# A streaming-encoder kernel: idle products at the start, x on another queue, a new order of the first splits

## The chip, the cores and the metric

The kernel runs on one core of a Trainium2 chip. A core has five engines that run at the same time, each doing its own instructions strictly in their order: TensorE (PE in the profile; PEld are its weight loads), VectorE (DVE), ScalarE (ACT), GpSimd (POOL) and SyncE (SP). Engines wait for each other, and for transfers (DMA), by semaphores. The metric is the device time of one execution in microseconds (us); less is better.

## What is computed

Two layers over 256 positions of width 1024, each of three sub-layers with a layer norm behind each. The first and third sub-layer are gated feed-forward parts with 2816 inner channels, the second is a diagonal state-space mixer (S5) in layer 0 and a gated spatial mixer in layer 1. Everything is float32.

```python
def _swiglu(x, w_in, w_out):
    gate, up = jnp.split(x @ w_in, 2, axis=-1)
    return (jax.nn.silu(gate) * up) @ w_out

for i in range(2):
    h = _layernorm(ALPHA * h + 0.5 * _swiglu(h, ffn_w_in[i, 0], ffn_w_out[i, 0]), ...)
    mix = _s5_mixer(h, ...) if i == 0 else _gmlp_mixer(h, ...)
    h = _layernorm(ALPHA * h + mix, ...)
    h = _layernorm(ALPHA * h + 0.5 * _swiglu(h, ffn_w_in[i, 1], ffn_w_out[i, 1]), ...)

# in the S5 mixer, from its small parameters
dt = jnp.exp(log_dt)                       # step sizes
mag = jnp.exp(a_re * dt); lam = mag * (cos(a_im * dt), sin(a_im * dt))
bbar = (lam - 1) / a * b                   # then a scan over positions with lam
```

## The kernel before

**Products in two parts.** Each float32 operand is split into a high part (a cast, on ACT) and a low part (the difference, on DVE), and a product is two or three PE products of parts: high by high, high by low, low by high. So each weight has to pass ACT and DVE before PE can use it.

**The weight stream.** Class `Stream` brings all weights in blocks of 128 x 2048 values (1 MB), numbered here from 0 in the order of use. `load` issues a block's transfers on SP's queue into one of three raw buffers (`N_RAW`); a raw buffer is free again when its block's low part is made. `split` makes the parts, into one of five pairs of split buffers (`N_SPLIT`), free again when PE has used the block. `tick` is called by the program after each group of PE products: it finishes what is unfinished, loads, splits up to n blocks, and does one step of background work. With `lazy` set, a tick casts the high part and leaves the low part to the next tick.

**The first feed-forward sub-layer** goes in eleven chunks of 256 inner channels. The blocks are: 0 and 1 for chunk 0, 2 and 3 for chunk 1, 4 and 5 for chunk 2, then for each further chunk c one block of the output weights of chunk c - 3 and two of its input weights: 6, then 7 and 8 for chunk 3, and so on to 24, then 25 and 26 for chunk 9. `start_in` does chunk 0 by itself, in quarters of a block as they come in (lines named L106 and L107 in the profile, `split_pieces`): it turns x by PE transposes (`make_xt`, L187, parts on ACT and DVE at L192 and L193) and multiplies (`in_mm`, L201 to L203, one group of three products for each of the eight slices k of the width and each half t of the positions). Then `chunk_in(1)` and onward, whose products are the lines L208 to L210, four groups of 24 products a chunk, each group followed by a tick; from chunk 2 on each chunk is followed by the output products of the chunk two before it (`step_out`).

**x.** Its first 128 positions (`h[0]`) are loaded by SP in two halves ahead of the weights; the second 128 (`h[1]`) stand among the quarters of block 0, behind its second quarter.

**The preparation of the S5 mixer** runs as background work under this first sub-layer, a list of steps (`add(first, cost, f)`): a step is done in order when the count of ticks has reached `first` and credit is left. It begins with `turn_a`, called as `ws.early` in `start_in`: small PE transposes of the parameters (L751, L752) and copies of them on ACT (L748 to L763). Then come the exponential for the step sizes `dt` in three pieces on DVE (L717, L721), `scaled` on POOL (L711, `ch<-ch,dt`), 32 small loads of B and 16 of C issued by POOL (L908, L977), rotation factors by repeated squaring on POOL (`seed`), a base table on POOL (`base_table`), rows for B on DVE (`b_rows`, with factors that go out to memory and come back by `spread`), and from tick 20 on tables made on DVE from a copy of the base table on ACT (`table`, L887 is that copy `tb<-base`), then products (`product`, `pq`).

The order of all this is fixed by the program as written; nothing is planned while it runs.

Of the kernel before, what the change touches and what calls it, by code (L numbers as in the profile page):

```python
# [9 lines left out]
F32 = mybir.dt.float32  # L10
# [6 lines left out]
P = 128  # L17
# [137 lines left out]
def hybrid(ctx: ExitStack, tc: tile.TileContext, a: dict, out: bass.AP, subs=SUBS):  # L155
# [186 lines left out]
    def plan_ffn(li, fi, fine):  # L342
        w_in, w_out = a["ffn_w_in"][li, fi], a["ffn_w_out"][li, fi]
        ids = {"in": {}, "out": {}}

        def add_in(c):

            ids["in"][c] = []
            for kh in range(2):
                parts = []  # L350
                step = 1 if fine and c == 0 else 4
                for k in range(0, 4, step):
                    row = 512 * kh + P * k
                    src = w_in[row:row + P * step, :].rearrange("(k p) (g n) -> p k g n", p=P, g=2)[:, :, :, c * FC:c * FC + FC]
                    dst = lambda raw, k=k, step=step: raw.rearrange("p (k g n) -> p k g n", k=4, g=2)[:, k:k + step]
                    if step == 1:
                        parts.append((lambda raw, dst=dst: dst(raw)[:, 0], src[:, 0]))
                    else:
                        for g in range(2):
                            parts.append((lambda raw, dst=dst, g=g: dst(raw)[:, :, g], src[:, :, g]))  # L360
                if step == 1 and kh == 0:
                    parts[2:2] = [(lambda raw: h[1], a["x"][0, P:2 * P, :])]
                ids["in"][c].append(ws.add(*parts))

        add_in(0)
        add_in(1)
        for c in range(2, NCH):
            add_in(c)
            ids["out"][c - 2] = add_rows(w_out, (c - 2) * FC)
        for c in (NCH - 2, NCH - 1):  # L370
            ids["out"][c] = add_rows(w_out, c * FC)
        return ids

    def ffn(ids, li, si, first, last):
# [42 lines left out]
        def chunk_in(c):  # L417

            for m in range(2):
                ps = mm_p.tile([P, 2, SEQ], F32, tag="mm", name="ips")  # L420
                for g in range(2):
# [10 lines left out]
                        finish_g()  # L432
                    if (m, g) == (1, 1) and c == NCH - 1:
                        split_gt()
                    ws.tick()

        def chunk_in2(c):

# [34 lines left out]
        def split_gt():  # L473
            while later:
                x, g = later.pop()
                nc.scalar.copy(x[:, 0], g)  # L476
                nc.vector.tensor_tensor(x[:, 1], g, x[:, 0].bitcast(F32), op=ALU.subtract)  # L477

        def start_in():

            ps = [mm_p.tile([P, 512], F32, tag="mm", name="ips") for _ in range(2)]
            mm = lambda t, k: in_mm(ids["in"][0], t, ps[t], [k])
            make_xt(0, parts=[0])
            split = ws.split_pieces(4)
            split(0)
            make_xt(0, parts=[1])
            mm(0, 0)
            split(1)
            make_xt(1)
            ws.early()  # L490
            mm(0, 1)
            for k in range(2):
                mm(1, k)
            for k in range(2, 4):
                split(k)
                for t in range(2):
                    mm(t, k)
            split = ws.split_pieces(4)
            for k in range(4):
                split(k)  # L500
                for t in range(2):
                    mm(t, 4 + k)
                if k >= 2:
                    ws.tick(0)
# [23 lines left out]

        if first:
            start_in()  # L530
            ws.lazy = True
            chunk_in(1)
        else:
            step_in(0, 0, split=0)
# [157 lines left out]
    def prepare_s5(sm, qp, dram):  # L692
# [326 lines left out]
        loads()  # L1019
        ws.early = turn_a  # L1020
        for cost, f in exp(lambda: val["ldt"], "dt"):
            add(1, cost, f)
        add(2, 0, scaled)
        for part in range(4):
            add(2, 0, load_b, part)
# [334 lines left out]
    with tc.manual_schedule():  # L1360
# [8 lines left out]
        kinds = [k for k, _, _ in subs]  # L1369
        for n in range(2):  # L1370
            s = slice(512 * n, 512 * n + 512)
            nc.sync.dma_start(out=h[0][:, s], in_=a["x"][0, 0:P, s])
        if kinds[0] != "ffn":
            nc.sync.dma_start(out=h[1], in_=a["x"][0, P:2 * P, :])
        ws.fill()
        if kinds[0] != "ffn":
            make_xt(0, kinds[0] == "s5")
# [52 lines left out]
```

## Time and profile before

| | us |
|---|---|
| median of 3 runs | 956.26 |
| lowest, highest | 956.1, 958.12 |
| profiled execution | 957.04 |
| its span in the profile | 955.2 |

| engine | busy, share of the span |
|---|---|
| PE | 937.7 us, 98% |
| DVE | 693.5 us, 73% |
| ACT | 466.9 us, 49% |
| POOL | 155.7 us, 16% |

In rows in order of time the first number is the start in us from the span's start, the second the duration (of all instructions that the row merges, from the first's start to the last's end), then engine, line, operation, output<-input, the shape and the count. Behind it, in brackets, stands how long the engine had been idle and what released it. In a row of a stretch, each engine's busy us stand in the order that the row above names, then the granted PE clock and the transfers. A row of waits gives who waited for whom, the sum, how often and the longest. A row of transfers ends with the KB of one and the median us from issue to landing.

### The profile page before, as it was taken

How to read it: one execution, taken by the hardware profiler on the slowest of the kernel's cores; microseconds unless marked ns; L12 is line 12 of the kernel's file. 1: busy time of each engine (PE TensorE's matmuls, PEld its weight loads, DVE VectorE, ACT ScalarE, POOL GpSimd, SP SyncE). 2: the span in 40 equal slices, each digit the busy share in tenths (PEclk: the TensorE clock that was granted, in tenths of full speed). 3: DMA queues.
4: the chain of work that ended last, by engine and by line, in shares of the span. 5: the costliest groups of instructions: out<-in, count | busy, mean ns of one | idle time of the engine just before them, and what ended most of it. 6: DMA issues, size and time to landing. Idle time of an engine off the chain costs nothing.

```text
span 955.2 us, 15164 instructions
## 1 busy us (share of the span) xinstructions
PE 937.7 (98%) x6142; PEld 813.9 (85%) x6142; DVE 693.5 (73%) x930; ACT 466.9 (49%) x612; POOL 155.7 (16%) x228
## 2 busy tenths in 40 slices
PE   7999999999999999999999999999999999999996
PEld 6999999978898888888888888888889888888885
DVE  6789998787999766564677756556789867564655
ACT  5475347534334464545534645454445445545540
POOL 1878911001652000000001000000000000000000
PEclk9999999999999999999999999999999999999999
DMA  8787696858637657465557674646357467565521
GB/s 280 208 244 251 219 313 218 293 202 322 221 124 242 197 178 248 149 215 181 176 176 243 222 262 161 228 140 221 132 176 265 132 201 233 184 219 178 182 84 45
DMA packets 134038, 195.02 MB, mean 204 GB/s; under 512 B 7648, under 2 KB 104848, under 8 KB 133968
## 3 DMA queue, kind: packets, MB, share of 16 engines
q1 hardware_dynamic: 129296, 182.74, 58.1%
q0 software_dynamic: 4384, 10.92, 3.9%
q8 instruction: 48, 0.79, 0.3%
q10 hardware_dynamic: 288, 0.39, 0.1%
q14 instruction: 22, 0.18, 0.1%
HBM read 184.07 MB, written 9.96 MB: 203 GB/s over the span
## 4 chain that ended last, share of the span: by engine, by line
PE 75%; DVE 2%; ACT 1%; POOL 0%; issue 0%; DVEq 0%; POOLq 0%; ACTq 0%
PE ips L216 21%; PE ips L217 11%; PE acc L203 8%; PE acc L201 8%; PE acc L202 8%; PE ips L203 2%; PE ips L201 2%; PE ips L202 2%; PE pps L1152 2%; PE tps L187 1%; PE zps L210 1%; PE zps L209 1%; PE zps L208 1%; PE ups L203 1%; PE ups L201 1%; PE ups L202 1%
## 5 line engine op out<-in xcount | busy, mean ns | idle before, releaser
L216 PE MATMUL ips<-xt,hi 128*128 128x512 f32 x864 | 306.2, 398 | 0.0
L89 DVE TENSOR_TENSOR lo<-raw,hi 128x2048 fp32r<-128x2048 f32 x107 | 243.1, 2294 | 8.2 <-ACT hi L88 8.0
L217 PE MATMUL ips<-xt,lo 128*128 128x256 f32 x864 | 242.5, 281 | 0.0
L88 ACT CAST hi<-raw 128x2048 fp32r<-128x2048 f32 x107 | 204.3, 1912 | 43.8 <-PE acc L203 25.3
L216 PEld LDWEIGHTS ips<-xt,hi 128*128 128x128 f32 x864 | 162.3, 188 | 39.9
L217 PEld LDWEIGHTS ips<-xt,lo 128*128 128x128 f32 x864 | 163.1, 189 | 1.1
L201 PE MATMUL acc<-hi,gt 128*128 128x512 f32 x346 | 136.2, 394 | 0.5 <-ACT gt L476 0.5
L451 DVE TENSOR_TENSOR sgg<-sgg,ips 128x256 f32<-128x256 f32 x108 | 45.5, 421 | 124.5 <-ACT sgg L450 124.1
L203 PE MATMUL acc<-hi,gt 128*128 128x512 f32 x346 | 135.1, 391 | 0.0
L202 PE MATMUL acc<-lo,gt 128*128 128x512 f32 x346 | 134.9, 390 | 0.0
L229 POOL TENSOR_TENSOR rstd<-rstd,mhalf 128x1 f32<-128x1 f32 x14 | 13.3, 950 | 619.7 <-DVE rstd L228 619.7
L97 DVE TENSOR_TENSOR lo<-raw,hi 128x2048 fp32r<-128x2048 f32 (+2 forms) x52 | 89.8, 1754 | 24.8 <-ACT hi L96 24.6
L450 ACT COPY sgg<-ips 128x256 f32<-128x256 f32 x108 | 40.3, 373 | 115.7 <-PE ips L217 115.7
L210 PE MATMUL ips<-xt,lo 128*128 128x256 f32 x320 | 90.7, 284 | 2.1 <-DVE lo L89 2.1
L208 PE MATMUL ips<-xt,hi 128*128 128x256 f32 x320 | 90.8, 284 | 0.0
L209 PE MATMUL ips<-xt,hi 128*128 128x256 f32 x320 | 90.5, 283 | 0.0
L201 PEld LDWEIGHTS acc<-hi,gt 128*128 128x128 f32 x346 | 65.0, 188 | 14.7 <-ACT gt L476 1.3
L203 PEld LDWEIGHTS acc<-hi,gt 128*128 128x128 f32 x346 | 64.9, 188 | 14.7 <-DVE gt L477 0.3
L96 ACT CAST hi<-raw 128x2048 fp32r<-128x2048 f32 (+2 forms) x52 | 74.9, 1484 | 2.6 <-DMA raw<-in_ffn_w_in 2.3
L202 PEld LDWEIGHTS acc<-lo,gt 128*128 128x128 f32 x346 | 65.1, 188 | 12.4
L477 DVE TENSOR_TENSOR gt<-sgg,gt 128x256 fp32r<-128x256 f32 x74 | 32.2, 435 | 51.2 <-ACT gt L476 51.2
L476 ACT CAST gt<-sgg 128x256 fp32r<-128x256 f32 x74 | 30.0, 406 | 70.7 <-DVE sgg L468 43.6
(251 smaller groups left out, 1524.5 us busy)
## 6 DMA issues: line engine op xcount, KB each, us to landing
raw<-in_ffn_w_in SPq DMA_DIRECT2D x172, 512.0 KB, 5.2
raw<-in_ffn_w_out SPq DMA_DIRECT2D x44, 1024.0 KB, 5.1
raw<-in_g_w_in SPq DMA_DIRECT2D x8, 1024.0 KB, 5.1
rows<-w SPq DMA_DIRECT2D x8, 512.0 KB, 6.5
raw<-in_s_w_in SPq DMA_DIRECT2D x4, 1024.0 KB, 8.2
raw<-in_s_w_glu SPq DMA_DIRECT2D x4, 1024.0 KB, 5.0
w<-rows SPq DMA_DIRECT2D x8, 512.0 KB, 5.8
tc<-tc SPq DMA_DIRECT2D x16, 256.0 KB, 5.4
```

Of the source, the lines that this page charges most:

```text
L88: nc.scalar.copy(hi, raw)
L89: self.unfinished.append(lambda: nc.vector.tensor_tensor(lo, raw, hi.bitcast(F32), op=ALU.subtract))
L96: nc.scalar.copy(hi[:, s], raw[:, s])
L97: eng[p % len(eng)].tensor_tensor(lo[:, s], raw[:, s], hi[:, s].bitcast(F32), op=ALU.subtract)
L201: nc.tensor.matmul(ps, xh, wh, start=start, stop=False)
L202: nc.tensor.matmul(ps, xh, wl, start=False, stop=False)
L203: nc.tensor.matmul(ps, xl, wh, start=False, stop=stop)
L208: nc.tensor.matmul(ps, wh, xh, start=start, stop=False)
L209: nc.tensor.matmul(ps, wh, xl, start=False, stop=False)
L210: nc.tensor.matmul(ps, wl, xh, start=False, stop=stop)
L216: nc.tensor.matmul(both, wh, xt[:, :, :, k].rearrange("p t j c -> p j t c"), start=k == 0, stop=False)
L217: nc.tensor.matmul(ps[:, 0], wl, xt[:, :, 0, k], start=False, stop=k == KD - 1)
```

## The change

Five edits. Two runs of idle products, seven and two, multiply zeros into a PSUM tile that nobody reads, before and behind the first transposes of x. All of x is issued on ACT's queue, so SP's queue begins with the weights. In `start_in` the four quarters of block 0 are split one after another, the first two slices are multiplied for the first 128 positions, and the second 128 positions are turned after that; the small S5 transposes come behind the first slice of block 1. Blocks 4 and 5 are both split, high and low, in the first tick of chunk 1. The exponential for the step sizes may begin at tick 3, not 1.

```diff
@@ plan_ffn
-                if step == 1 and kh == 0:
-                    parts[2:2] = [(lambda raw: h[1], a["x"][0, P:2 * P, :])]
@@ chunk_in
-                    ws.tick()
+                    if first and (c, m, g) == (1, 0, 0):
+                        ws.tick(2)
+                        ws.lazy = True
+                    else:
+                        ws.tick()
@@ ffn
+        def idle(n):
+
+            ps = mm_p.tile([P, 512], F32, tag="mm", name="idle")
+            for _ in range(n):
+                nc.tensor.matmul(ps, zero, zero.unsqueeze(1).broadcast_to([P, 4, P]), start=True, stop=True)
+
         def start_in():
...
+            idle(7)
             make_xt(0, parts=[0])
             split = ws.split_pieces(4)
             split(0)
             make_xt(0, parts=[1])
+            idle(2)
+            split(1)
             mm(0, 0)
-            split(1)
-            make_xt(1)
-            ws.early()
             mm(0, 1)
-            for k in range(2):
-                mm(1, k)
             for k in range(2, 4):
                 split(k)
-                for t in range(2):
-                    mm(t, k)
+            make_xt(1)
+            for k in range(2, 4):
+                mm(0, k)
+            for k in range(4):
+                mm(1, k)
             split = ws.split_pieces(4)
             for k in range(4):
                 split(k)
+                if k == 1:
+                    ws.early()
                 for t in range(2):
                     mm(t, 4 + k)
@@ ffn, first sub-layer
             start_in()
-            ws.lazy = True
             chunk_in(1)
@@ prepare_s5
         for cost, f in exp(lambda: val["ldt"], "dt"):
-            add(1, cost, f)
+            add(3, cost, f)
@@ hybrid
-            nc.sync.dma_start(out=h[0][:, s], in_=a["x"][0, 0:P, s])
-        if kinds[0] != "ffn":
-            nc.sync.dma_start(out=h[1], in_=a["x"][0, P:2 * P, :])
+            nc.scalar.dma_start(out=h[0][:, s], in_=a["x"][0, 0:P, s])
+        nc.scalar.dma_start(out=h[1], in_=a["x"][0, P:2 * P, :])
```

How this moves the instructions, at three places. First PE's own start, before and then changed (`h_94` and `h_95` are the two halves of x, `tps` a tile of transposes, `aps` the small S5 transposes):

```order
L187 MATMUL tps<-ident,h_94 128x128 x8
L201 MATMUL ips<-hi_154,xt 128x512
L202 MATMUL ips<-lo_155,xt 128x512
L203 MATMUL ips<-hi_154,xt 128x512
L187 MATMUL tps<-ident,h_95 128x128 x8
L751 MATMUL aps<-ident,s5a 128x32 x3
L752 MATMUL aps<-ident,s5a 128x16
```

```order
L485 MATMUL idle<-zero 128x512 x7
L187 MATMUL tps<-ident,h_94 128x128 x8
L485 MATMUL idle<-zero 128x512 x2
L201 MATMUL ips<-hi_162,xt 128x512
L202 MATMUL ips<-lo_163,xt 128x512
L203 MATMUL ips<-hi_162,xt 128x512
```

In the changed order six products, not three, stand ahead of the second half's transposes, and the `aps` rows are gone from here: they stand 24 products behind those transposes.

Second, ACT around the copies of those small transposes, before and then changed (the casts of L106 are quarters of blocks 0 and 1, those of L96 whole blocks 2 and 3):

```order
L192 CAST xt<-tps 128x512 x2
L748 COPY s5a<-dt_131 32x128
L757 COPY ch<-aps 128x64
L759 COPY ldt<-aps 128x32
L762 COPY dg<-aps 128x8
L763 ACTIVATE dg<-aps 128x8
L106 CAST hi_154<-raw_101 128x512 x2
L106 CAST hi_222<-raw_107 128x512 x4
L96 CAST hi_274<-raw_112 128x2048
```

```order
L106 CAST hi_162<-raw_102 128x512 x3
L192 CAST xt<-tps 128x512 x2
L106 CAST hi_220<-raw_107 128x512 x2
L758 COPY s5a<-dt_131 32x128
L767 COPY ch<-aps 128x64
L769 COPY ldt<-aps 128x32
L772 COPY dg<-aps 128x8
L773 ACTIVATE dg<-aps 128x8
L106 CAST hi_220<-raw_107 128x512 x2
L96 CAST hi_273<-raw_112 128x2048
```

The copies moved behind the whole of block 0 and the first half of block 1; behind them stand two quarters instead of six.

Third, DVE behind the quarters of block 1, before and then changed (`ex` to `dt` and `ee` belong to the exponential, `lo_274` to `lo_325` are the low parts of blocks 2 to 5, `sgg` the gate of a chunk, `gt` its turned pieces):

```order
L717 TENSOR_SCALAR ex<-ldt 128x32
L717 TENSOR_SCALAR ek<-ex 128x32
...
L721 SCALAR_TENSOR_TENSOR dt<-dt,er 128x32 x6
L97 TENSOR_TENSOR lo_275<-raw_112,hi_274 128x2048
L97 TENSOR_TENSOR lo_282<-raw_248,hi_281 128x2048
L717 TENSOR_SCALAR ee<-ek 128x32
...
L711 TENSOR_TENSOR dt<-dt,ee 128x32
L399 TENSOR_TENSOR sgg<-ips,sgg 128x256 x2
```

```order
L97 TENSOR_TENSOR lo_274<-raw_112,hi_273 128x2048
L97 TENSOR_TENSOR lo_281<-raw_259,hi_280 128x2048
L397 TENSOR_TENSOR sgg<-ips,sgg 128x256 x2
L97 TENSOR_TENSOR lo_318<-raw_262,hi_317 128x2048
L97 TENSOR_TENSOR lo_325<-raw_277,hi_324 128x2048
L727 TENSOR_SCALAR ex<-ldt 128x32
...
L731 SCALAR_TENSOR_TENSOR dt<-dt,er 128x32 x6
L470 TENSOR_TENSOR sgg<-ips,sgg 128x256
L391 TENSOR_TENSOR gt<-tps,gt 128x128 x4
L727 TENSOR_SCALAR ee<-ek 128x32
```

The low parts of four blocks stand ahead of the exponential, and its last piece, `ee` and what follows, stands behind the gate and the turned pieces of the next chunk. Later steps of the preparation keep their order; their places among the blocks move by a tick or so, among them the base table's first use, which comes behind block 20 instead of ahead of it, and the product groups (`pq`), which from the second on come one place later among the blocks.

## The prediction

> **What bounds the kernel now.** I read the page's busy times first, then the busy time by stretch, then the rows in order of time where TensorE (PE) stands still.
>
> ```profile
> PE 937.7 (98%) x6142; PEld 813.9 (85%) x6142; DVE 693.5 (73%) x930; ACT 466.9 (49%) x612; POOL 155.7 (16%) x228
> ...
> core 0: us, PE busy (x) PEld busy (x) DVE busy (x) ACT busy (x) POOL busy (x), PEclk, DMA share, GB/s
> 0.00:24.80 24.80, 19.79 (x68) 15.14 (x69) 15.21 (x32) 13.89 (x22) 3.59 (x13) 1.00 0.88 281
> 24.80:60.00 35.20, 33.73 (x259) 32.53 (x258) 26.36 (x80) 20.96 (x27) 27.89 (x49) 1.00 0.88 222
> 60.00:145.00 85.00, 85.00 (x603) 80.21 (x602) 83.81 (x110) 39.04 (x45) 59.73 (x92) 1.00 0.82 259
> ```
>
> PE is busy for 98% of the span, so a gain must come from places where it waits or runs slowly, and all places of this change lie in the first 40 us. But the last row holds the second bound: from 60 to 145 us DVE is busy for 83.81 of 85.00 us. There it makes the low halves of the weights and, between them, the S5 preparation. Time won before 60 us reaches the end only if DVE and its suppliers come along.
>
> ```profile
> 0.73 0.86 SPq L1372 DMA_DIRECT2D h<-in_x  x2
> ...
> 0.88 0.20 POOL L172 MEMSET zero<- 128x128 f32 x1
> ...
> 1.65 1.29 SPq L63 DMA_DIRECT2D raw<-in_ffn_w_in  x2
> ...
> 4.15 1.94 PE L187 MATMUL tps<-ident,h 128*128 128x128 f32 x8 [4.15 <-DMA h<-in_x]
> ...
> 8.46 1.97 PE L187 MATMUL tps<-ident,h 128*128 128x128 f32 x8
> ...
> 17.33 0.61 PE L202 MATMUL ips<-lo,xt 128*128 128x512 f32 x1
> 17.75 0.42 PE L203 MATMUL ips<-hi,xt 128*128 128x512 f32 x1
> 18.01 0.39 PE L201 MATMUL ips<-hi,xt 128*128 128x512 f32 x1
> 18.23 0.39 PE L202 MATMUL ips<-lo,xt 128*128 128x512 f32 x1
> ...
> 24.83 0.28 PE L208 MATMUL ips<-xt,hi 128*128 128x256 f32 x1
> 24.95 0.28 PE L209 MATMUL ips<-xt,hi 128*128 128x256 f32 x1
> ...
> 40.08 0.39 PE L210 MATMUL ips<-xt,lo 128*128 128x256 f32 x1 [1.47 <-DVE lo L89]
> ```
>
> PE waits 4.15 us for x (rows here and below are picked, in order of time). Up to 17.75 a 512-wide product starts 0.42 us after the one before it, afterwards 0.22 to 0.23, though the granted clock reads 1.00: PE starts at half speed and turns fast there. Chunk 1 begins at 24.83. At 40.08 chunk 2 has waited 1.47 us for the low half of block 5.
>
> **The change, part by part.** The sum is made against the profiled execution, 957.04 us (a span of 955.2 and 1.84 around it), which is 0.78 above the median of 956.26.
>
> *The start of PE.* Zeros are ready at 1.08. Seven idle products at the slow 0.42 take 2.9 us, to about 4.2; they fill time in which PE waited for x. x now shares the transfer engines with the first weights: it lands between 4.15 (no sharing) and 5.1 (its first half lets a quarter block of 256 KB pass at 281 GB/s, 0.93 us). I take 4.3, nearer the row, since a half of x is issued in 0.43 us (0.86 for two) and a quarter block in 0.65. Eight transposes 1.94, to 6.2; two idle products 0.85, to 7.1. From there I take PE as fast. Three products 0.7, to 7.8; the next three wait for a low half (two casts on ACT, two low parts on DVE, 0.5 to 0.6 each by the rows below, behind those of the turned x) until about 8.4, to 8.9; the transposes of x's second half at twice their speed 1.0, to 9.9; 24 products at 0.227 (30 from 18.01 to 24.83) 5.5, to 15.4; the small transposes of the S5 parameters 0.3, to 15.7.
>
> By the Trainium skill ("TensorE: Matmul & The Clock Gate", The HAM clock gate) PE's default is half clock, released after some 3.4 us of sustained work seen in a free-running window. Work from 1.25 on would then release it between 4.7 and 8.1, and at the later end the first three products cost at most 0.6 us more; whether transposes count as work that section doesn't say, and the trace had 6.3 us of products and transposes from 4.15 on without becoming fast.
>
> What waits there is the chain behind those small transposes:
>
> ```profile
> 11.72 0.21 ACT L757 COPY ch<-aps 128x64 f32<-128x64 f32 x1 [0.48 <-PE aps L752]
> ...
> 12.04 3.23 ACT L106 CAST hi<-raw 128x512 fp32r<-128x512 f32 x6
> ...
> 12.71 3.71 DVE L107 TENSOR_TENSOR lo<-raw,hi 128x512 fp32r<-128x512 f32 x6 [0.93 <-ACT hi L106]
> ...
> 16.33 0.18 DVE L717 TENSOR_SCALAR ex<-ldt 128x32 f32<-128x32 f32 x1
> ...
> 18.88 2.29 DVE L97 TENSOR_TENSOR lo<-raw,hi 128x2048 fp32r<-128x2048 f32 x1
> ...
> 19.44 1.92 ACT L96 CAST hi<-raw 128x2048 fp32r<-128x2048 f32 x1 [1.71 <-DMA raw<-in_ffn_w_in]
> ...
> 23.59 0.17 DVE L717 TENSOR_SCALAR ee<-ek 128x32 f32<-128x32 f32 x1
> ...
> 25.06 0.32 POOL L711 TENSOR_TENSOR ch<-ch,dt 128x64 f32<-128x64 f32 x1 [20.83 <-DVE dt L711]
> ...
> 31.48 0.43 DVE L468 TENSOR_TENSOR sgg<-ips,sgg 128x256 f32<-128x256 f32 x1 [3.39 <-ACT sgg L467]
> ...
> 33.26 0.29 DVE L393 TENSOR_TENSOR gt<-tps,gt 128x128 fp32r<-128x128 f32 x1 [0.33 <-ACT gt L392]
> ...
> raw<-in_ffn_w_in SPq DMA_DIRECT2D x8, 512.0 KB, 5.3
> ...
> h<-in_x SPq DMA_DIRECT2D x2, 256.0 KB, 3.4
> ```
>
> ACT's four copies of these transposes now stand ahead of the last two high quarters of block 1, and ACT does its rows in order. From 15.7: copies 0.3 (11.72 to 12.04), two quarters 1.1 (six in 3.23), blocks 2 and 3 at 1.9 each, to 20.9; DVE's low halves (2.29, overlapping a little where they follow each other, so 2.2) end at 21.2 and 23.4. In the trace of before the same chain waited for the transfer instead (19.44), so transfers don't hold it now. PE, with 18 products left (4.1), comes to chunk 1 at 19.8, waits for both low halves, and finishes the first quarter of the chunk at 23.4 + 1.3 = 24.7; before it was 24.83 + 2.88 (24 products at 0.12) = 27.7. That is **3.0 won**. Splitting blocks 4 and 5 at once puts block 5's low half at 31.0 (below), before PE, in chunk 2 from 33.7, needs it, so the 1.47 goes too: PE is **4.5 us** ahead in chunk 2.
>
> *The step from 1 to 3.* The exponential of the step sizes (16.33 to 18.88, 2.55 us, and its end, 23.59 to 24.8, 1.2 us) now stands on DVE behind the low halves of blocks 4 and 5. Block 5 can be loaded when block 2's buffer is free, 21.2; its issue takes 0.4 and its transfer 5.3, to 26.9; high 1.9, low 2.2, to 31.0. Then 2.55, the gate and four turned pieces 2.1 (31.48 to 33.55), 1.2: the step sizes are there at 36.8, and POOL, which needs them, starts at 37.0 instead of 25.06: **11.9 us later**. What stands behind it on POOL is 32 small loads of B, 16 of C, the rotation factors and their base table.
>
> ```profile
> POOL bq L908 <- DMA bq<-in_s_b_re: 2.6, 3, 1.2
> ...
> POOL cz L977 <- DMA cz<-in_s_c_re: 2.3, 3, 1.1
> ...
> 113.40 0.80 POOL L711 TENSOR_TENSOR base<-base,bt 128x256 f32<-128x256 f32 x1
> ...
> 114.23 0.41 ACT L887 COPY tb<-base 128x256 f32<-128x256 f32 x1 [0.91 <-POOL base L711]
> ...
> 119.61 0.75 DVE L711 TENSOR_TENSOR tx<-tb,ch 128x256 f32<-128x256 f32 x2
> ...
> 120.80 2.29 DVE L89 TENSOR_TENSOR lo<-raw,hi 128x2048 fp32r<-128x2048 f32 x1
> ...
> 144.19 0.69 DVE L711 TENSOR_TENSOR pq<-pq 128x512 f32<-128x512 f32 x1
> ...
> 146.61 0.42 DVE L468 TENSOR_TENSOR sgg<-ips,sgg 128x256 f32<-128x256 f32 x1 [1.39 <-ACT sgg L467]
> ...
> 157.47 2.29 DVE L89 TENSOR_TENSOR lo<-raw,hi 128x2048 fp32r<-128x2048 f32 x1
> ...
> 159.82 0.39 PE L210 MATMUL ips<-xt,lo 128*128 128x256 f32 x1 [0.63 <-DVE lo L89]
> ```
>
> POOL's chain from 25.06 ended with the table at 114.20, and ACT already waited 0.91 us for it; DVE came to its tables at 119.61 and had no more idle time than 1.39 us until the low half of block 26, for which PE waited 0.63 us at 159.82. With the same 89.1 us of chain the table is there at 126.1, the copy at 126.5, and DVE, ready earlier, waits. From there to the end of block 26 it has 40.15 us (119.61 to 159.76) less 1.39 idle, less 2.2 for block 20, now ahead of the tables, less 2.0 for one product group (144.19 is the last of its three rows), now behind block 26: 34.8. Block 26 is ready at 161.3 instead of 159.76: PE loses its 4.5 and **1.5 more**. I find no such wait behind it in this sub-layer, so the loss stays to the end.
>
> *The bounds.* POOL's start: 35.0 if block 5 lands after 3.4 us, as x did, and x at 4.15; 39.3 if x lands at 5.1 and PE turns fast 3 us later. Its chain: the loads' waits (the first two rows above, 4.9 us) may go or double. From the low ends the table is there at 119.2; then DVE's own arrival decides: 119.61, plus 2.55 (the exponential) and 2.2 (block 20), less the idle it saves between 24.8 and 60 (8.84 now; I see about 3.5 left around blocks 4 and 5, and as much for the B products, whose factors come back from memory later), 122.5. Block 26 is then ready at 157.3, 2.5 us won; if that second wait stays away, all 4.5. From the high ends: table at 133.3, a loss of 8.7. I keep the middle value of each term: **+1.5**, 958.5 for the profiled execution, 957.8 for the median.
>
> *At no cost:* ACT's three issues (0.4 to 0.6 each, as SP's) and its table load end before x lands; without that cover each issue adds its 0.4 at the start. By the Trainium skill ("DMA: Bandwidth & Descriptors", Issuing engines are not separate DMA queues) a second issuing engine gives no bandwidth, both interleave on the same 16 engines: this speaks against moving x, and by it x lands at 5.1 and the start takes 0.8 more. No run shown has the two queues side by side.
>
> **Rivals.** *The early gain gets through:* POOL's chain is shorter by 4 us or more, or starts by 34. For it: 4.9 us of it are waits and DVE would run ahead. Against it: it has to make up all 11.9 less the 5 that lie between 114.64 and 119.61, and DVE's 83.81 of 85.00. It gives 2.5 won, 953.8 for the median, 951.8 with the whole 4.5.
> *PE stays slow* until 17.75, as before: idle products and transposes don't turn it fast. For it: 4.15 to 10.43 didn't, transposes in it included. Against it: idle products are of the shape that did. From 7.1 on six products take 2.5 and eight transposes 1.97; 14 of the 24 products are done by 17.75, the rest ends at 19.9, the small transposes at 20.2, 4.5 us later than in the sum. POOL then starts at 41.5 and block 26 is ready at 165.8, 6.0 lost: 962.3. This chain turns to a loss where the table comes after 124.5 (159.76 - 34.8 - 0.4).
> *The parameters' chain doesn't matter, nor the start:* both move by under 1 us; 956.3.
>
> **How the numbers follow.** The late table has 0.5 (its own range 955.5 to 960.5), the gain getting through 0.32 (951.8 to 955), PE staying slow 0.1 (959.5 to 963), nothing moving 0.08. Faster or slower by over 0.2% (1.9 us, what a measurement here can tell) means under 954.35 or over 958.17. Faster: 0.26 of the 0.32. Slower: 0.25 of the late table's half and all of the slow clock's 0.1, 0.35. Same: 0.39. The range reaches from the middle of the second case to half of the slow clock's, 952.7 to 961.
>
> **What would show it.** Right: PE's 0.23 step by 8 us, chunk 1 at 20 with waits for DVE's low halves, no wait at chunk 2; POOL's first product at 37; ACT waiting many us for the base table near 110 to 126, DVE behind it, and PE waiting for low halves between 115 and 160. Wrong: no wait of PE on DVE in that stretch (then the early gain stays), or a step of 0.42 after 12 us.

## The result: slower by 0.9%

The changed kernel takes 965.71 us (median of 4 runs, 963.71 to 967.36), the kernel before, measured beside it, 956.18 (4 runs). The ratio is 1.0087, with a 95% interval of 1.0071 to 1.0103: 6.8 to 9.8 us slower. The prediction was 957.8, in a range of 952.7 to 961.0, and the measured time lies outside it. The profiled execution took 965.98 us with a span of 964.2, against 955.2 before: 9.0 us more.

### The profile page after: what moved, and what is told of

The parts are those of the page before. It is cut to its first block, busy times and chain, and to the rows that moved or that the text cites. A ratio compares the mean times of both kernels' runs of the same rounds, so it can differ in the third digit from the quotient of the medians.

```text
span 964.2 us, 15189 instructions
## 1 busy us (share of the span) xinstructions
PE 938.9 (97%) x6151; PEld 814.9 (85%) x6151; DVE 693.8 (72%) x930; ACT 466.9 (48%) x612; POOL 155.6 (16%) x228
## 4 chain that ended last, share of the span: by engine, by line
PE 77%; DVE 3%; ACT 1%; issue 0%; POOL 0%; DVEq 0%; POOLq 0%; ACTq 0%
PE ips L216 21%; PE ips L217 11%; PE acc L203 8%; PE acc L201 8%; PE acc L202 8%; PE ips L201 2%; PE ips L203 2%; PE ips L202 2%; PE pps L1162 2%; PE zps L210 1%; PE zps L209 1%; PE zps L208 1%; PE ups L203 1%; PE tps L187 1%; PE ups L201 1%; PE ups L202 1%
## 5 line engine op out<-in xcount | busy, mean ns | idle before, releaser
L89 DVE TENSOR_TENSOR lo<-raw,hi 128x2048 fp32r<-128x2048 f32 x105 | 238.8, 2295 | 4.2 <-ACT hi L88 4.2
L88 ACT CAST hi<-raw 128x2048 fp32r<-128x2048 f32 x105 | 200.6, 1915 | 27.3 <-PE acc L203 25.0
L217 PEld LDWEIGHTS ips<-xt,lo 128*128 128x128 f32 x864 | 163.1, 189 | 1.1
L97 DVE TENSOR_TENSOR lo<-raw,hi 128x2048 fp32r<-128x2048 f32 (+2 forms) x54 | 94.3, 1775 | 30.0 <-ACT hi L96 29.9
L96 ACT CAST hi<-raw 128x2048 fp32r<-128x2048 f32 (+2 forms) x54 | 78.8, 1502 | 4.4 <-DMA raw<-in_ffn_w_in 3.3
L210 PEld LDWEIGHTS ips<-xt,lo 128*128 128x128 f32 x320 | 62.1, 194 | 5.9 <-DVE lo L89 4.0
```

Source lines behind the costliest of these rows:

```text
L88: nc.scalar.copy(hi, raw)
L89: self.unfinished.append(lambda: nc.vector.tensor_tensor(lo, raw, hi.bitcast(F32), op=ALU.subtract))
L96: nc.scalar.copy(hi[:, s], raw[:, s])
L97: eng[p % len(eng)].tensor_tensor(lo[:, s], raw[:, s], hi[:, s].bitcast(F32), op=ALU.subtract)
L210: nc.tensor.matmul(ps, wl, xh, start=False, stop=stop)
L217: nc.tensor.matmul(ps[:, 0], wl, xt[:, :, 0, k], start=False, stop=k == KD - 1)
```

## The profile after

The stretches of the changed kernel, with the columns of the prediction's table (busy time and instructions of each engine, then granted clock, DMA share, GB/s):

```profile
0.00:24.80 24.80, 20.47 (x90) 15.41 (x91) 11.45 (x14) 14.02 (x23) 3.60 (x13) 1.00 0.79 256
24.80:60.00 35.20, 33.66 (x257) 32.30 (x257) 28.34 (x82) 16.53 (x22) 17.16 (x31) 1.00 0.77 221
60.00:145.00 85.00, 79.46 (x545) 74.26 (x544) 77.20 (x111) 40.69 (x46) 67.05 (x106) 0.98 0.80 238
```

Up to 60 us PE is as busy as before. From 60 to 145 it does 545 instructions where it did 603, and DVE, which was busy for 83.81 us, is busy for 77.20. PE loses its time there and later, well behind the part of the program that the change touches.

The start, in order of time (rows picked):

```profile
8.95 1.35 ACT L106 CAST hi<-raw 128x512 fp32r<-128x512 f32 x2 [1.98 <-DMA raw<-in_ffn_w_in]
12.26 0.39 PE L203 MATMUL ips<-hi,xt 128*128 128x512 f32 x1
12.49 0.39 PE L201 MATMUL ips<-hi,xt 128*128 128x512 f32 x1
17.34 0.37 PE L761 MATMUL aps<-ident,s5a 32*128 32x32 f32 x3
18.78 1.29 DVE L107 TENSOR_TENSOR lo<-raw,hi 128x512 fp32r<-128x512 f32 x2 [4.12 <-ACT hi L106]
22.16 0.28 PE L208 MATMUL ips<-xt,hi 128*128 128x256 f32 x1
25.66 0.39 PE L210 MATMUL ips<-xt,lo 128*128 128x256 f32 x1 [0.52 <-DVE lo L97]
37.20 0.39 PE L208 MATMUL ips<-xt,hi 128*128 128x256 f32 x1 [1.02 <-DVE sgg L470]
40.17 0.32 POOL L721 TENSOR_TENSOR ch<-ch,dt 128x64 f32<-128x64 f32 x1 [35.94 <-DVE dt L721]
```

PE is fast (a product 0.23 behind the one before it) from 12 us on, and comes to chunk 1 at 22.16, 2.67 earlier than before in these two executions. Most of that goes at once, since the low halves of blocks 2 and 3 come late. In chunk 2 PE is 1.19 us ahead. POOL's first product of the preparation starts at 40.17 instead of 25.06.

What PE, DVE and ACT wait for between 60 and 145 us (total us, number of waits, longest):

```profile
ACT tb L897 <- POOL base L721: 7.4, 1, 7.4
DVE prod L721 <- DMA fac<-cf: 7.0, 1, 7.0
PE ips L210 <- DVE lo L89: 3.1, 2, 1.8
PE acc L202 <- DVE lo L89: 2.4, 1, 2.4
```

Before, PE had no wait in this stretch and ACT 0.9 us for the base table; DVE had none for `fac`. The new wait of DVE in order of time, and what follows on PE up to 195 us:

```profile
65.87 2.28 DVE L89 TENSOR_TENSOR lo<-raw,hi 128x2048 fp32r<-128x2048 f32 x1
75.16 1.35 DVE L721 TENSOR_TENSOR prod<-bq,fac 128x512 f32<-128x512 f32 x2 [7.01 <-DMA fac<-cf]
85.58 0.50 PE L202 MATMUL acc<-lo,gt 128*128 128x512 f32 x1 [2.41 <-DVE lo L89]
94.14 0.39 PE L210 MATMUL ips<-xt,lo 128*128 128x256 f32 x1 [1.36 <-DVE lo L89]
130.24 0.39 PE L210 MATMUL ips<-xt,lo 128*128 128x256 f32 x1 [1.76 <-DVE lo L89]
177.08 1.36 PE L1017 MATMUL kps<-cl,bar 128*32 128x32 f32 x120 [1.32 <-ACT cl L963]
184.64 0.40 PE L202 MATMUL acc<-lo,gt 128*128 128x512 f32 x1 [2.91 <-DVE pq L721]
```

`fac` are the factors for the rows of B, which `spread` sends out to memory and fetches back in another layout. Their way out, back and to DVE's first use, in the kernel before and then in the changed one:

```profile
54.37 0.34 SPq L844 DMA_DIRECT2D cf<-fac  x1
59.12 6.85 DVE L89 TENSOR_TENSOR lo<-raw,hi 128x2048 fp32r<-128x2048 f32 x3
61.60 1.76 SPq L848 DMA_DIRECT2D fac<-cf  x4
65.89 1.35 DVE L711 TENSOR_TENSOR prod<-bq,fac 128x512 f32<-128x512 f32 x2
```

```profile
62.45 0.34 SPq L854 DMA_DIRECT2D cf<-fac  x1
68.23 1.76 SPq L858 DMA_DIRECT2D fac<-cf  x4
```

They leave 8.1 us later than before, the fetch is issued 6.6 later, and it takes 5.5 us to land (median of its four transfers) where it took 1.8. DVE comes to its first use only 2.3 us later than before (68.15), and the program gives it nothing else to do there: it stands idle for 7.01 us, and the low halves behind it are late. By these figures about half of that wait (3.7 us) goes with the slower landing. How far PE is behind the kernel before, by the start of the same product in both traces:

| place | before | changed | behind |
|---|---|---|---|
| chunk 1, first product | 24.83 | 22.16 | -2.67 |
| chunk 2, second quarter | 41.37 | 40.18 | -1.19 |
| chunk 4, last quarter | 81.09 | 79.90 | -1.19 |
| chunk 6, first product | 106.41 | 109.54 | +3.13 |
| chunk 8, first product | 140.37 | 147.14 | +6.77 |
| chunk 10, first product | 178.74 | 189.87 | +11.13 |
| last output product in that stretch | 209.13 | 218.39 | +9.26 |

## Experiments

Two theories at first. **A**: the step from tick 1 to 3 of the exponential carries all of the loss, through the chain of the S5 parameters. **B**: the new order of the first splits does, by where the low halves stand on DVE. Ratios are of the run to the kernel before measured beside it, with 95% intervals; one thousandth is about 1 us.

### One edit undone, one edit alone

```diff
 after_exp1, in the changed kernel
-            add(3, cost, f)
+            add(1, cost, f)

 before_exp3, in the kernel before
-            add(1, cost, f)
+            add(3, cost, f)
```

> The changed kernel with one edit undone: the exponential of the step sizes may begin at tick 1 again, not 3. Theory A (this edit alone carries the loss, through POOL's chain of the S5 parameters): the exponential's first two pieces (2.55 us) stand on DVE ahead of the low halves of blocks 2 and 3, so those come about 1.5 us later than in the changed kernel and about all of the early gain goes, but the step sizes are there near 28.4 and POOL starts near 28.6 instead of 40.17; the base table is complete near 117, DVE waits at most 1 us for the factors that go through memory (7.01 in the changed kernel), and the time is 954 to 957. Theory B (the other order of the first splits and the two blocks split at once carry it, by the places of the low halves on DVE): POOL is early as well, but PE's waits for low halves between 83 and 131 us stay, and the time is 962 to 966.

> The kernel before with one edit alone: the exponential of the step sizes may begin at tick 3, not 1. Theory A (this edit alone carries the loss): POOL's first product moves from 25.06 to about 37.4, the base table from 114.2 to about 126.5; DVE waits several us for the factors out of memory and PE for low halves behind that; since the early gain of 1.2 us is missing, 964 to 967. Theory B (other edits carry the loss): POOL is as late, but no new wait of PE above 1 us comes between 60 and 160, and the time stays within 955.5 to 957.5.

Measured: with the step undone 1.0003 (0.9990 to 1.0016), no difference; with the step alone 1.0080 (1.0067 to 1.0093), as slow as the whole change. The step carries the loss, and the other four edits together are worth nothing that can be measured (a gain and a cost that cancel, as after_early below shows). That is theory A; B had both the other way. In the kernel before with the step alone, DVE's wait for the factors from 60 to 145 us is that of the changed kernel, and ACT's for the base table about half of it:

```profile
DVE prod L711 <- DMA fac<-cf: 7.2, 1, 7.2
ACT hi L88 <- DMA raw<-in_ffn_w_in: 5.1, 2, 3.9
ACT tb L887 <- POOL base L711: 3.9, 1, 3.9
```

The median of after_exp1, 957.76, is above what theory A had for it (954 to 957), but so was the kernel before beside it, 957.90. Its profile has PE at half clock twice in the start; that is taken up under the hardware.

### The two waits, taken away one by one

```diff
 after_no_trip: no trip of the factors through memory
         def spread(back):
             if not back:
-                nc.sync.dma_start(out=res["cf"], in_=...)
                 A.copy(val["bf"], val["cf"][T - 1])
-                return
-            for t in range(T):
-                nc.sync.dma_start(out=val["cqs"][...], in_=res["cf"][...])
 ...
+            V.memset(val["cqs"], 0.5)

 after_no_base: tables not begun from POOL's base table
-                A.copy(val["tb"][:, :, :, 0:16], val["base"][:, :, q])
+                A.copy(val["tb"][:, :, :, 0:16], h[0].rearrange(...)[:, :, q])

 after_no_both: both
```

> The changed kernel, in which the factors for the rows of B do not go out to memory and back: the 32 turned sets of factors are filled with the constant 0.5 when the first factors are made (so rows of B and all that follows from them are not the reference's; five transfers are left out, every other instruction stays). It takes away DVE's wait of 7.01 us for that trip and nothing else. Theory A1 (that wait is the price): DVE's work stands 7 us earlier from 68 us on, PE's waits between 83 and 131 go and stay away, 957.5 to 959.5. Theory A2 (POOL's late base table takes its place at once): ACT's first copy of the table stays at 128, DVE comes to the tables 7 us early and waits there until 128.4 instead, the low halves behind that are only 1 to 2 us earlier than in the changed kernel, and 962.5 to 964.5.

> The changed kernel, in which ACT's four copies that begin the tables read a part of x that lies ready, not POOL's base table (so the tables and what follows from them are not the reference's; POOL still makes the base table, and the trip of the factors through memory is left as it is). It takes away ACT's wait of 7.4 us for the base table alone. Theory A3 (the trip has taken DVE's time already, and the table's lateness is hidden behind that): DVE's 7 us wait and PE's waits between 83 and 131 stay, ACT's wait goes, and the time is 963 to 966. Theory A4 (the table alone is the price, as predicted): PE's waits after 115 go and the time is 957 to 960.

> The changed kernel with both taken away: the factors do not go through memory (a constant stands in their place) and the tables begin from a part of x, not from POOL's base table (rows of B and tables are not the reference's). Theory A (a late start of POOL's chain costs by these two waits and by nothing else): PE keeps its lead of 1.2 us over the kernel before through chunk 8, and the time is 955 to 958, no change against the kernel before. Rival E (something else that the late step sizes or the other order move costs as well, the products with C and their copies behind 165 us): PE falls behind from 165 on, 959 to 963.

In these three runs the rows of B, the tables or both are not those of the computation. Measured: without the trip 1.0071 (1.0051 to 1.0091); without the wait for the base table 1.0088 (1.0072 to 1.0105); without both 1.0048 (1.0028 to 1.0069). Without the trip PE keeps its lead of 1.2 us until 134 us. Then comes this (waits of that kernel from 60 to 145 us, and two rows of its timeline):

```profile
ACT tb L893 <- POOL base L721: 12.7, 1, 12.7
DVE tx L721 <- ACT tb L893: 5.3, 1, 5.3
PE acc L202 <- DVE lo L89: 4.0, 1, 4.0
```

```profile
127.51 0.41 ACT L893 COPY tb<-base 128x256 f32<-128x256 f32 x1 [12.70 <-POOL base L721]
127.95 0.76 DVE L721 TENSOR_TENSOR tx<-tb,ch 128x256 f32<-128x256 f32 x2 [5.26 <-ACT tb L893]
```

The base table takes the place of the trip, as theory A2 said: DVE, now early at its tables, waits there for 5.26 us. The other way round nothing changes at all, as A3 said: in the changed kernel ACT's 7.4 us for the base table lie behind the time that the trip has cost already. Taken alone, neither wait makes a difference that these intervals show against the change's 1.0071 to 1.0103; both together do.

But it doesn't go away. After_no_both was forecast by theory A at no change, 955 to 958; it took 961.84, in the bounds of rival E (959 to 963). E had PE fall behind from 165 us on; it is 0.8 us behind the kernel before at chunk 8 (141.15 against 140.37) and 3.8 at the last output product. Theory A was incomplete: with the chain's two waits gone, 0.3% to 0.7% stayed.

### What is left: DVE's time

In that kernel DVE has no wait above 1.2 us from 44 to 145 us, yet PE falls behind from 134 us on. DVE's own row shows why. These are the changed kernel without both waits, then the kernel before, in two stretches:

```profile
14.00:40.00 26.00, 24.00 (x160) 21.23 (x159) 15.44 (x29) 12.86 (x19) 0.00 (x0) 1.00 0.79 255
40.00:136.00 96.00, 94.98 (x683) 89.88 (x682) 91.75 (x162) 50.32 (x57) 85.04 (x136) 1.00 0.77 231
```

```profile
14.00:40.00 26.00, 24.61 (x155) 22.30 (x153) 20.26 (x53) 14.72 (x20) 14.29 (x26) 1.00 0.74 208
40.00:136.00 96.00, 95.92 (x687) 90.96 (x688) 91.04 (x147) 47.98 (x50) 70.05 (x111) 1.00 0.85 250
```

From 40 us on DVE is full in both (91.75 and 91.04 of 96). From 14 to 40 it does 20.26 us of work in the kernel before and 15.44 here, because it waits for high halves:

```profile
19.86 1.29 DVE L107 TENSOR_TENSOR lo<-raw,hi 128x512 fp32r<-128x512 f32 x2 [5.43 <-ACT hi L106]
22.19 4.49 DVE L97 TENSOR_TENSOR lo<-raw,hi 128x2048 fp32r<-128x2048 f32 x2 [1.03 <-ACT hi L96]
28.76 2.29 DVE L97 TENSOR_TENSOR lo<-raw,hi 128x2048 fp32r<-128x2048 f32 x1 [1.41 <-ACT hi L96]
32.62 2.29 DVE L97 TENSOR_TENSOR lo<-raw,hi 128x2048 fp32r<-128x2048 f32 x1 [1.57 <-ACT hi L96]
```

The first of these waits is not the step's: after_exp1 has it too (4.30 us until 20.01), since ACT makes these high halves behind the copies of the small transposes, which the change put there. The other three, 4.01 us, are time that the exponential could fill. It may not begin yet, and its work comes later, where DVE has no time to spare. **Theory G**: DVE is the bound from about 40 to 165 us, so what counts is the work that it has done by then, and each microsecond that it loses ends on PE, unless the work fills time in which it waits anyway. Three runs test that. Two add the same work on DVE, which nobody reads, to the kernel before, once where DVE waits anyway and once where it is full; one leaves work out (the rows of B of the fourth part, so the computation is changed there).

```diff
 before_dve_early and before_dve_late
+        def extra():
+            x = ln_p.tile([P, D], F32, tag="r", name="extra", bufs=2)
+            for _ in range(4):
+                tt(x, h[0], h[0], MUL)
 early: behind the first piece of the second exponential
+            if n == 0:
+                add(3, 0, extra)
 late: ahead of the rows of B of the second part
+                if (j, part) == (0, 1):
+                    add(13, 0, extra)

 after_no_both_less
-                add(13, 1.9, b_rows, j, part)
+                if part < 3:
+                    add(13, 1.9, b_rows, j, part)
+                else:
+                    add(13, 1.9, lambda: None)
```

> The kernel before with four products of 128 x 1024 on DVE that nobody reads (about 1.15 us each by half of the low half's 2.29, 4.6 in all), put ahead of the rows of B of the second part, near 75 us. Theory G (DVE is the bound from about 60 to 165, so each microsecond that it loses there, by waiting or by work, ends on PE): the low halves of the blocks from 12 on come 4.6 us later, PE's one wait at block 26 grows and new ones come, and the time is 3.5 to 5 us over the kernel before of the same call. Rival H (the low halves' slack of 2 to 6 us at blocks 12 to 23 takes it up): less than 1.5 us over.

> The kernel before with the same four products on DVE, put behind the first piece of the second exponential, near 28 us, where DVE waits 3.39 us for PE's chunk 1. Theory G: 3.4 of the 4.6 us fill the wait, block 5's low half and so PE's stall in chunk 2 come about 1.2 us later, and the time is 0 to 1.5 us over the kernel before of the same call. Rival (what DVE does early delays the parameters' chain by its whole length): 3.5 us and more over.

> The changed kernel with both waits taken away, as in an earlier run (no trip of the factors through memory, tables begun from a part of x), and in addition without the products and sums for the rows of B of the fourth part, eight instructions on DVE between 108 and 117, 4.6 us (2.23 and 2.41; these rows are then left as the third part's). What was left of the loss there was 4 to 5 us, with no wait of DVE above 1.2 us between 44 and 145. Theory G (DVE is the bound there, and the 8.5 us in which it stands idle between 14 and 33, for want of the exponential that now comes later, are the rest of the loss): taking as much of DVE's work away as is left of the loss brings the time down by 3.5 to 4.8 us against that run's 0.48% over the kernel before, to at most 0.15% over it. Rival (the rest is lost in the products with C and their copies from 165 on, whatever DVE does before): within 1.5 us of that run, 0.3% and more over the kernel before.

Measured: late 1.0060 (1.0044 to 1.0075), early 1.0024 (1.0015 to 1.0034), less 1.0000 (0.9985 to 1.0014). The late work is 5.09 us in the trace, not 4.6, and costs 4.2 to 7.2, where G had 3.5 to 5 and H less than 1.5. The early work is 5.00 and costs 1.4 to 3.3, nearly all of it above G's 0 to 1.5 and below the rival's 3.5: G's size was too low there. PE waited 2.52 and 1.30 us in chunk 2 and ran at half clock from 38 to about 45 us, which G had not counted. So by the middle values (5.7 and 2.3) the same work costs more than twice as much where DVE is full as where it waits. Leaving out 4.6 us of DVE's work took away all that was left of the loss, as G had it. That the unfilled time before 40 us is what left DVE behind is read from the two stretches; no run filled that time in this kernel and changed nothing else.

DVE's busy time from 14 to 136 us against the span, each as a difference to the profiled execution of the kernel before (111.30 and 955.2). Where work was added to DVE or left out in the stretch, the first number is corrected for it (but for the filling with constants, 0.27 us in the three runs without the trip):

| run | DVE work by 136 us | span |
|---|---|---|
| the change | -9.0 | +9.0 |
| before_exp3 | -7.4 | +9.3 |
| after_no_idle (below) | -8.9 | +9.1 |
| after_no_base | -9.4 | +9.4 |
| after_no_trip | -8.7 | +5.5 |
| before_dve_late | -5.3 | +6.9 |
| after_no_both | -4.1 | +4.1 |
| before_dve_early | -1.8 | +1.2 |
| after_exp1 | -0.9 | +0.3 |
| after_no_both_less | +0.2 | +0.9 |
| after_early_no_idle (below) | +1.6 | +0.2 |
| after_early_lazy (below) | +2.2 | -2.0 |
| after_early (below) | +2.3 | -1.7 |

The two go together within 2 us but for after_no_trip, whose span grew by 3.2 us less than DVE lost; DVE's wait came as late as 122 us there, and the low halves may have had that much lead over PE, which no run tested. A table of this kind shows only that they move together; the cause is in the three runs above.

### The idle products, and a version that is faster

```diff
 after_no_idle, in the changed kernel
-            idle(7)
 ...
-            idle(2)

 after_early: the changed kernel with the exponential at tick 1 and
             make_xt(1)
+            ws.early()
             for k in range(2, 4):
                 mm(0, k)
 ...
                 split(k)
-                if k == 1:
-                    ws.early()

 after_early_no_idle: that, without idle(7) and idle(2)
 after_early_lazy: that, with chunk 1's ticks as the kernel before has them
```

> The changed kernel without the nine idle products. Theory C (they bring PE to the fast step, and the start then needs it): the step of the 24 products that follow the second half's transposes is 0.427 us until about 17.75 instead of 0.2275 throughout, the small S5 transposes come near 20.6 instead of 17.34, all that waits for them is 2.9 us later, POOL starts near 43 instead of 40.17, and the time is 967 to 969.5. Rival D (the step turns fast at the same time by x's own transposes and the first products, or PE waits for low halves anyway): the same step and 964.5 to 966.5.

> The changed kernel with the exponential at tick 1 and the small transposes of the S5 parameters right behind the second half of x, where the kernel before has them, not behind the first slice of block 1. ACT's copies of them then wait for PE only until about 12.8, block 1's last high quarters come near 15 instead of 18.1, the exponential stands on DVE while it would wait for block 2, and POOL starts near 24 (before 25.06). Theory A (only the late chain ate the early gain): the first quarter of chunk 1 ends near 25 (before 27.6), PE is 2 to 3.5 us ahead in chunk 2 and keeps part of it to the end, 952 to 955.5. Rival F (DVE, busy 83.81 of 85 us between 60 and 145, is the bound there and the early gain is given back whatever POOL does): 955.5 to 957.5.

> As the run before it (exponential at tick 1, small transposes early), but with blocks 4 and 5 split as the kernel before does: one block a tick, low half one tick later, from chunk 1 on. What the double split is worth then shows. If it takes away the stall at block 5 (1.47 us in the kernel before), this is 1 to 2 us slower than the run before it, with a wait of PE of 1 us or more in the first quarter of chunk 2; if PE's lead is given back later anyway, both have the same time within 0.7 us.

> The run with the exponential at tick 1 and the small transposes early, without the nine idle products. Theory D' (x's transposes and the first products bring PE to the fast step by about 12.7, as without idle products in the changed kernel; PE then comes to chunk 1 about 1 us later): 0 to 1.5 us slower than with them. Rival C' (here PE is the bound of the start, nothing else hides its slow step): the first quarter of chunk 1 ends 2 to 3 us later and the time is 2 to 3 us slower than with them.

Measured: without idle products in the changed kernel 1.0081 (1.0068 to 1.0094), which cannot be told from the changed kernel with them: rival D. PE was fast there from 12.69 on, without them, and came to chunk 1 at 23.24, 1.08 later than with them, which cost nothing that can be measured.

With the exponential and the small transposes early: 0.9975 (0.9961 to 0.9989), that is 1 to 4 us **faster than the kernel before**, 954.93 us in the median, as theory A had it and rival F had not. POOL starts at 24.76, DVE has done 21.52 us of work between 14 and 40, and PE is 4.2 us ahead of the kernel before from chunk 2 to chunk 8. After_exp1 differs from it only in the small transposes, which stand behind the first slice of block 1 there: 1.0003 (0.9990 to 1.0016) against 0.9975 (0.9961 to 0.9989). So that one place in the order costs some 1 to 5 us, and the change has the costlier one. With the ticks of chunk 1 as before it is 0.9977 (0.9964 to 0.9991): the double split of blocks 4 and 5 is worth nothing here, though PE does wait 1.61 us for block 5 without it; the forecast of 1 to 2 us for it was wrong, and its other branch, that the lead is given back later, is what happened. Without idle products 0.9984 (0.9967 to 1.0001), and the two intervals overlap: what the idle products are worth in this version, up to some 2 us or nothing, stays open. Where after_early gives its lead back:

```profile
148.58 0.50 PE L202 MATMUL acc<-lo,gt 128*128 128x512 f32 x1 [0.46 <-DVE lo L89]
156.85 0.39 PE L210 MATMUL ips<-xt,lo 128*128 128x256 f32 x1 [1.09 <-DVE lo L89]
191.22 0.50 PE L201 MATMUL acc<-hi,gt 128*128 128x512 f32 x1 [1.01 <-ACT gt L478]
204.42 1.23 PE L187 MATMUL tps<-ident,h 128*128 128x128 f32 x8 [0.80 <-DVE h L238]
```

The first two are DVE's bound again. PE is 4.2 us ahead in front of them, 2.96 behind block 26, and 1.81 at the last output product of that stretch.

## Why the prediction was wrong, by its steps

**What bounds the kernel now: right, and not followed.** The prediction named DVE as the second bound from 60 to 145 us (83.81 of 85.00) and said that time won early reaches the end only if DVE and its suppliers come along. Then it priced the change by the times at which things are ready, with the base table as the only thing that DVE would wait for, and not by how much of DVE's work is done when it becomes the bound. That is the step that failed; what it missed is in the two paragraphs on DVE below.

**The start of PE: fast early, but the cause not shown, and the size off.** PE turned fast as forecast (0.23 by 12 us at the latest). That the idle products did it isn't shown: without them it was fast by 12.69. Transposes of x began at 4.29, as the sum had it (4.3). The second slice of block 0 was cast from 8.95 on, with 1.98 us of waiting for its transfer, where the kernel before cast it at 7.05; the sum had PE's second three products at 8.4, and they began at 9.62. The small transposes came at 17.34 instead of 15.7. So the low halves of blocks 2 and 3 ended at 23.3 and 25.6 instead of 21.2 and 23.4, and of the "3.0 won" 0.77 was left, in these two executions.

**The stall of chunk 2: off.** Block 5's low half was ready at 34.3, before PE needed it, and the 1.47 went. But the first product of chunk 2 waited 1.02 us for a gate (`sgg`) that DVE does behind the two low halves and the exponential. PE was 1.19 ahead, not 4.5. That leaves 3.3 us less to lose before a loss shows.

**The step from 1 to 3: right in kind, low in size.** POOL's start was put at 37.0 and came at 40.17 (above the upper bound of 39.3), because block 5's low half came at 34.3, not 31.0. The chain behind it was put at 89.1 us and took 87.9: the base table was there at 128.04, not 126.1, and ACT waited 7.4 us for it, as the prediction said it would show.

**"DVE, ready earlier, waits": wrong.** DVE didn't wait for the base table at all. It had waited for the factors, for 7.01 us, 50 us earlier. The prediction followed the parameters' chain along POOL to the base table and left out its other arm, along DVE: step sizes, second exponential, factors, out to memory and back, rows of B. Of that arm it had one half sentence, in the bounds ("as much for the B products, whose factors come back from memory later", about 3.5). That was half of what the wait came to, and it served only the low end of the range. The trace of before had the rows, shown above: the factors leave at 54.37, the fetch is issued from 61.60 on and takes 1.8 us to land, and DVE's first use stood at 65.89 behind three low halves. By these rows there was about 1 us of room.

**"1.5 more": wrong by 7.5 us.** The profiled span grew by 9.0. Of these, both waits together hold 3.7 to 4.9 (4.9 by the spans of the change and after_no_both, 0.39% or 3.7 by their ratios), and the rest is DVE's unfilled time before 40 us. In its middle value the prediction gave that no price: the exponential's 3.75 us were put down as standing "behind the low halves", as a delay of POOL, and not as work that leaves a place where DVE waits for one where it is full. Only the low end counted 2.55 of them on DVE, and set 1.84 of saved idle time against them. Two of its sums are also off, too little to matter: 40.15 less 1.39, 2.2 and 2.0 is 34.6, not 34.8, and the middle of 951.8 to 955 is 953.4, not the 952.7 at which the range begins.

**The rivals and the range.** The rival on the slow side had PE's slow start as its cause, which didn't come: PE was fast by 12 us. (In the profile of after_early_no_idle it was slow until 18.78, and that run was no slower than the kernel before.) "The early gain gets through" needed a chain shorter by 4 us or a start of POOL by 34; it was 1.2 shorter and started at 40.17. The bounds of the late table reached a loss of 8.7 us; that case was given no weight of its own and the range ended at 961. It would have come near the result by luck, since DVE never waited for the table in the changed kernel.

## What to carry to other kernels

Where two engines are nearly full, price a moved piece of work on each of them twice: what it delays, and whether the place that it leaves would have been idle and the place that it goes to is full. A wait taken away from a late chain shows its price only if the next wait of the same chain isn't ready to take its place: take away all of them at once, too, and see what is left. And follow every arm of a chain to its first use, also those that pass through memory; the slack is in the row of the first use, between the landing and the end of the instruction before it, and the landing itself can move (1.8 us became 5.5 here).

## What the runs showed of the hardware

**PE lost its clock behind some waits shorter than 3 us.** In the changed kernel PE waited 1.76 us until 130.24. Soon after, the granted clock (third number from the end) falls for about 3.4 us, and the 24 products of a quarter that take 2.88 us take 4.37:

```profile
130.00:132.00 2.00, 1.76 (x13) 1.76 (x14) 1.97 (x7) 0.24 (x1) 2.00 (x2) 0.92 1.03 337
132.00:134.00 2.00, 2.00 (x12) 2.00 (x11) 1.97 (x6) 2.00 (x4) 2.00 (x2) 0.50 1.06 383
134.00:136.00 2.00, 2.00 (x14) 2.00 (x14) 1.97 (x7) 0.93 (x3) 0.93 (x1) 0.73 1.14 363
136.00:138.00 2.00, 2.00 (x19) 2.00 (x18) 1.97 (x6) 2.00 (x3) 0.00 (x0) 1.00 1.09 197
```

In after_exp1 it is the wait of 2.32 us in chunk 1's first quarter, until 26.12, behind which PE loses another 1.8 us (its clock had already been at 0.50 from 10 to 12 us, behind a wait of 1.43 until 9.50):

```profile
26.00:28.00 2.00, 1.88 (x11) 1.88 (x12) 2.00 (x2) 1.42 (x2) 0.00 (x0) 0.68 0.36 83
28.00:30.00 2.00, 2.00 (x11) 1.96 (x11) 1.83 (x9) 0.57 (x1) 0.33 (x1) 0.50 1.02 324
30.00:32.00 2.00, 2.00 (x18) 2.00 (x18) 2.00 (x2) 0.00 (x0) 1.84 (x4) 0.97 1.08 402
```

The same after waits of 3.96 (after_no_trip) and 3.28 us (after_no_idle), each with 1.9 us on top. But not always: the waits of 2.41 us until 85.58 in the changed kernel and of 1.76 until 131.70 in after_no_base were followed by a clock of 1.00. So a wait of about 2 us cost PE here between 2 and 4. No run tested what brings it about. The Trainium skill ("TensorE: Matmul & The Clock Gate", HAM oscillation — how this bites in real kernels) has the mechanism, a window of about 3.4 us in which PE is watched, and idle gaps longer than that as what throttles it. The 3.4 us for which the clock is halved agree with the window; the gap doesn't, since waits of 1.76 and 2.32 us stood ahead of it here.

**When PE turns fast differs between executions.** Three whose instructions on PE are the same up to that point turned fast at 17.75 (the kernel before), at 18.37 (before_dve_late) and by 12.10 (before_dve_early), and chunk 1 began at 24.83, 26.11 and 22.47. The prediction took the 17.75 of one execution for a property of the kernel, and a difference of 2 us in the start of two profiles says nothing about an edit. The first row of the table of places above carries this chance too.
